# A depthwise convolution split by token parity: three half-length filters in place of 31 taps

## The chip, the cores and the metric

The kernel runs on one core of a Trainium2 chip. The metric is the device time of one launch in microseconds; the time given for a kernel is the median of its runs. The core's engines work side by side, each in the order of its own instruction stream: PE (TensorE, the matrix multiplier), DVE (VectorE), ACT (ScalarE), POOL (GpSimd) and SP (SyncE, which here only starts DMA transfers). They wait for each other through semaphores. SBUF is the core's working memory, PSUM the smaller memory into which PE writes its products.

## The reference

One layer of a decoder trunk over 1024 tokens with 1024 channels, in float32. Cut to what the change touches:

```python
h = rms_norm(x, attn_norm_w[l])
proj = h @ w_in[l]
q, k, v, u, g = jnp.split(proj, splits, axis=-1)
a = diff_attention(...)                       # 8 heads, q and k in two halves
y_a = rms_norm(a, ...) @ w_proj_attn[l]

u_a, u_b = jnp.split(u, 2, axis=-1)
c = causal_depthwise_conv(u_a * jax.nn.sigmoid(u_b), conv_w[l], conv_b[l])
c = jax.nn.silu(layer_norm(c, conv_ln_w[l], conv_ln_b[l]))
y_b = c @ w_proj_conv[l]

x = x + (g_a * y_a + g_b * y_b) @ w_out[l]
x = x + (silu(gate) * up) @ w_down[l]         # feed-forward, width 2816
```

The convolution works on each channel alone: token s of the output is the bias plus the sum over t = 0..30 of w[30-t] times token s-t of its input. The input is called u below, already gated (u_a times the sigmoid of u_b).

## The kernel before

**Layout and products.** Channels lie on the 128 partitions, tokens along the free axis, so that u and the convolution's output are eight tiles (c = 0..7) of 128 channels by 1024 tokens. A float32 matrix product is made of three matmuls on halves of the numbers: a high part (`whi`, a copy with rounding, ACT, line 120) and a low part (`wlo`, the difference, DVE line 125, or POOL line 131 while `low_by_pool` is set). Lines 168 to 170 are the three matmuls. Some products are formed as seven products of quarter blocks in place of eight (lines 981 and 489).

**The stages**, by the trace of the profiled execution: an opening up to 60 us; up to 270 us the first stage, in which u is projected and gated; up to 825 us attention, with the projections of q, k and the gates as filling; up to 1010 us the attention projection, the LayerNorm of the convolution and the convolution projection; up to 1100 us `w_out`; then the feed-forward part.

**How u is made.** `u_half` makes tile 0, `u_pair` (line 992) tiles 1 to 7. For each, PE writes seven products of 12 matmuls into three PSUM tiles a, b and c_, and between the products the results are drained: an ACT copy (lines 999 and following), DVE additions and multiplications (lines 1001, 1014, 1016, 1022), a multiplication on POOL (line 1018). The sums of weight blocks for the seven products are made by POOL (lines 962 to 965), which makes the low halves there too. The two halves of tile c (512 tokens each) go to a DRAM buffer `u_d[c]` by DMAs of SP (lines 1019, 1023).

**How the convolution is made.** `conv_load` (line 574) brings tile c back whole to SBUF (`us[c]`, two buffers). `conv_taps` returns 31 work items for a tile: `first_tap` on ACT (line 589: scale by the tap, add the bias, write `acc`), then 30 taps on DVE (line 595), each of which multiplies the first 1024-n tokens of u by a per-channel weight `cw` and adds them in place to the last 1024-n tokens of `acc`. For the first four tiles (`CONV_PSUM`) `acc` lies in PSUM, and after the last tap ACT copies it to an SBUF tile `done` (line 599); for the others it lies in SBUF. The finished tile goes to `c_d[c]` by a DMA of SP (line 601), tile 0 also to `cs_d` (line 603); the other tiles are added to `cs_d` in DRAM by an accumulating DMA of POOL (`add_tile`, line 579). In all DVE makes 8 x 30 = 240 taps.

**When.** The items wait in a list `bg`. In the first stage each step of the main loop puts 3.25 of them into the program (line 1242, `due += 3.25`), each behind DVE's last instruction so far; at the end of the stage `bg.until` (line 1078) puts in more until 127 remain, that is until tiles 0 to 3 are done and tile 4 is loaded. In attention the rest is spread over the steps (`share`, line 1443). The DMA that loads the next tile is placed in the list so that it comes just after the first tap of the tile before. A list scheduler of the language's framework then orders each engine's stream when the kernel is built.

**After attention** `ln_chunks` (line 1544) runs the LayerNorm for each half of the tokens: it loads `cs_d` and the eight `c_d` tiles (lines 1554 and 1556, nine DMAs a half), takes the mean by a matmul, subtracts (line 1570), squares, divides, gates, and writes the high and low halves into `cT_hi` and `cT_lo` (lines 1593, 1594), from which PE makes the convolution projection.

Of the kernel before, what the change touches and what calls it, by code (L numbers as in the profile page):

```python
# [10 lines left out]
F32 = mybir.dt.float32  # L11
# [20 lines left out]
NT = S // P  # L32
NKT = D // P
NSTD = 2
SUMS = ("T1", "T2", "T3", "T4")
SIDES = ("11", "12", "22", "S1", "S2", "S3", "S4")

# [20 lines left out]
def kernel(  # L58
# [157 lines left out]
    NROW = 64  # L216
    rows = ap.tile([NROW, P], F32, name="rows", bufs=1)
    col = {}
    at = [0]
# [26 lines left out]

    pvec = cst.tile([P, NROW], F32, name="pvec")
    cw = cst.tile([P, NKT, 32], F32, name="cw")
    neglam = cst.tile([P, 1], F32, name="neglam")
    lprod = ap.tile([P, 2, HD], F32, name="lprod", bufs=1)  # L250
    lsum = cst.tile([P, 2], F32, name="lsum")

    def pcol(key, k=0):
        c = col[key] + k
        return pvec[:, c : c + 1]

    def vectors():

        pt = pm()
        pe.transpose(pt[:, :NROW], rows[:], ident[:NROW, :NROW])  # L260
        dve.tensor_copy(pvec[:], pt[:, :NROW])
        dve.tensor_scalar(pcol("subln"), pcol("subln"), 1.0 - LAM_INIT, None, op0=ALU.mult)
        dve.tensor_scalar(pcol("kn"), pcol("kn"), -(HD ** -0.5), None, op0=ALU.mult)
        c_ = col["ln_w"]
        dve.tensor_scalar(pvec[:, c_ : c_ + 8], pvec[:, c_ : c_ + 8], -0.125, None, op0=ALU.mult)
        pt = pm()
        for k in range(NKT):
            pe.transpose(pt[:, k * 32 : k * 32 + CW], cwrow[:, k * P : (k + 1) * P], ident[:CW, :CW])
        dve.tensor_copy(
            cw[:, :, :CW], pt[:, : NKT * 32].rearrange("p (k t) -> p k t", t=32)[:, :, :CW]  # L270
        )
        for j in range(2):
            dve.tensor_tensor(lprod[:, j, :], lamt[:, 2 * j, :], lamt[:, 2 * j + 1, :], op=ALU.mult)
        dve.tensor_reduce(lsum[:], lprod[:], axis=AX.X, op=ALU.add)
# [296 lines left out]
    def conv_load(c):  # L571
        def go():
            us[c] = cv.tile([P, S], F32, tag="u", name=f"u{c}", bufs=2)
            nc.sync.dma_start(us[c][:], u_d[c][:])

        return go

    def add_tile(c):
        pool.dma_start(cs_d[:], c_d[c][:], accum_op=ALU.add, max_dma_last_dim=1024)

    def conv_taps(c):
        acc = []

        def first_tap():
            if c < CONV_PSUM:
                acc.append(pcv[0].tile([P, S], F32, tag="acc", name=f"acc{c}", bufs=1))
            else:
                acc.append(cv.tile([P, S], F32, tag="acc", name=f"acc{c}", bufs=1))
            act.activation(acc[0][:], us[c][:], AF.Identity, bias=pcol("conv_b", c), scale=cw[:, c, CW - 1 : CW])  # L589

        def tap(t):
            def go():
                n = CW - 1 - t
                a_ = acc[0][:, n:]
                dve.scalar_tensor_tensor(a_, us[c][:, : S - n], cw[:, c, t : t + 1], a_, op0=ALU.mult, op1=ALU.add)  # L595
                if t == 0:
                    if c < CONV_PSUM:
                        done = cv.tile([P, S], F32, tag="acc", name=f"done{c}", bufs=1)
                        act.copy(done[:], acc[0][:])
                        acc[0] = done  # L600
                    nc.sync.dma_start(c_d[c][:], acc[0][:])
                    if c == 0:
                        nc.sync.dma_start(cs_d[:], acc[0][:])
                if c > 1 and t == CW // 2:
# [5 lines left out]
        return [first_tap] + [tap(t) for t in range(CW - 2, -1, -1)]  # L610

    hT_hi = big.tile([P, NKT, S], F32R, tag="xhi", name="hT_hi")
    hT_lo = big.tile([P, NKT, S], F32R, tag="xlo", name="hT_lo")


    def u_half(c, w, sb, gemm=gemm_T):
        cs = slice(sb * 512, (sb + 1) * 512)
        ob = gemm_T(w[0], hT_hi, hT_lo, sb)
        sg = wp.tile([P, 512], F32, tag="sg", name=nm("sg"), bufs=2)
        act.activation(sg[:], ob[:], AF.Sigmoid)  # L620
        yield
        oa = gemm(w[1], hT_hi, hT_lo, sb)
        dve.tensor_tensor(sg[:], oa[:], sg[:], op=ALU.mult)
        nc.sync.dma_start(u_d[c][:, cs], sg[:])
# [368 lines left out]
    def u_pair(c, A, ahead):  # L993

        B = {(j, l): (hT_hi[:, KH[j], TOK[l]], hT_lo[:, KH[j], TOK[l]]) for j in range(2) for l in range(2)}
        a, b, c_ = acc(), acc(), acc()
        product(b, A["11"], B[0, 0], True)
        p1 = half("p1")
        act.copy(p1, b[:])
        product(a, A["12"], B[1, 0], True)  # L1000
        dve.tensor_tensor(p1, a[:], p1, op=ALU.add)
        act.activation(p1, p1, AF.Sigmoid)
        nxt = next(ahead, None)
        yield
        product(b, A["S2"], TS[2], False)
        u2 = half("u2")
        act.copy(u2, b[:])
        product(c_, A["S1"], TS[1], True)
        u3 = half("u3")
        act.copy(u3, c_[:])  # L1010
        next(ahead, None)
        yield
        product(b, A["S3"], TS[3], False)
        dve.tensor_tensor(u3, b[:], u3, op=ALU.add)
        product(c_, A["S4"], B[1, 1], False)
        dve.tensor_tensor(u2, c_[:], u2, op=ALU.add)
        act.activation(u2, u2, AF.Sigmoid)
        pool.tensor_tensor(u3, u3, u2, op=ALU.mult)
        nc.sync.dma_start(u_d[c][:, TOK[1]], u3)
        yield  # L1020
        product(b, A["22"], TS[4], False)
        dve.tensor_tensor(p1, b[:], p1, op=ALU.mult)
        nc.sync.dma_start(u_d[c][:, TOK[0]], p1)
        bg.todo.insert(max(0, len(bg.todo) - CW), conv_load(c))
        bg.add(conv_taps(c))
        next(ahead, None)
        yield
        return nxt

    def first_stage():  # L1030
# [203 lines left out]
    for _ in first_stage():  # L1234
# [309 lines left out]
    def ln_chunks(sb):  # L1544
# [6 lines left out]

        s1 = half("s")
        with after(last_at):
            nc.sync.dma_start(s1[:], cs_d[:, cs])
# [32 lines left out]
        for c in range(NKT):  # L1587
# [540 lines left out]
```

## Time and profile before

| what | value |
| --- | --- |
| runs (us) | 1737.25, 1738.83, 1738.94 (median 1738.83) |
| profiled execution: time, span of its profile | 1738.77 us, 1737.0 us |
| PE busy | 1717.4 us, 99% of the span |
| DVE busy | 1275.2 us, 73% |
| ACT busy | 863.3 us, 50% |
| POOL busy | 218.6 us, 13% (nearly all of it before 270 us) |
| share of the chain that ended last | PE 89%, DVE 4%, DMA 3%, ACT 2%, POOL 1%, issue 1% |
| the 240 convolution taps on DVE | 303.8 us, 1266 ns each |

The span is the profile's own stretch from the first to the last instruction; the profiled execution took 1.77 us more than that. Busy times of different engines overlap. The chain that ended last is followed back from the last instruction, at each step to what released it. "x -> y" times are of one execution; means of one instruction are in ns.

### The profile page before, as it was taken

How to read it: one execution, taken by the hardware profiler on the slowest of the kernel's cores; microseconds unless marked ns; L12 is line 12 of the kernel's file. 1: busy time of each engine (PE TensorE's matmuls, PEld its weight loads, DVE VectorE, ACT ScalarE, POOL GpSimd, SP SyncE). 2: the span in 40 equal slices, each digit the busy share in tenths (PEclk: the TensorE clock that was granted, in tenths of full speed). 3: DMA queues.
4: the chain of work that ended last, by engine and by line, in shares of the span. 5: the costliest groups of instructions: out<-in, count | busy, mean ns of one | idle time of the engine just before them, and what ended most of it. 6: DMA issues, size and time to landing. Idle time of an engine off the chain costs nothing.

```text
span 1737.0 us, 25860 instructions
## 1 busy us (share of the span) xinstructions
PE 1717.4 (99%) x9245; PEld 1478.8 (85%) x9245; DVE 1275.2 (73%) x2128; ACT 863.3 (50%) x1958; POOL 218.6 (13%) x207
## 2 busy tenths in 40 slices
PE   9999999999999999999999999999999999999999
PEld 7997879998998998988788877888888888888887
DVE  7575879898988888878687768966676666565554
ACT  6333335667777777765566325633333333333332
POOL 4997761000000000000000000000000000000000
PEclk9999999999999999999999999999999999999999
DMA  6343546435435344443963683235445444598663
GB/s 202 118 133 121 178 137 166 117 92 146 117 109 148 108 116 128 105 134 132 337 234 122 200 302 104 74 105 180 152 158 174 154 152 150 175 361 280 216 218 132
DMA packets 260453, 281.64 MB, mean 162 GB/s; under 512 B 16418, under 2 KB 181858, under 8 KB 260324
## 3 DMA queue, kind: packets, MB, share of 16 engines
q1 hardware_dynamic: 254352, 269.55, 48.1%
q0 software_dynamic: 5680, 9.39, 2.5%
q8 instruction: 73, 1.20, 0.3%
q10 hardware_dynamic: 292, 1.05, 0.2%
q14 instruction: 56, 0.46, 0.1%
HBM read 181.84 MB, written 85.50 MB: 154 GB/s over the span
## 4 chain that ended last, share of the span: by engine, by line
PE 89%; DVE 4%; DMA 3%; ACT 2%; POOL 1%; issue 1%; SPq 0%; POOLq 0%
PE acc L981 28%; PE acc L489 12%; PE pg L168 12%; PE pg L169 11%; PE pg L170 11%; PE wo L1843 2%; PE sc L1290 2%; PE sc L1289 2%; PE pT L1328 2%; DVE acc L595 1%; PE pW L168 1%; PE pW L169 1%; PE pW L170 1%; PE pg L1107 1%; DMA wraw<-in_w_in_dram 1%
## 5 line engine op out<-in xcount | busy, mean ns | idle before, releaser
L595 DVE SCALAR_TENSOR_TENSOR acc<-u,cw,acc 128x1023 f32<-128x1023 f32 (+14 forms) x240 | 303.8, 1266 | 14.6 <-ACT acc L589 12.1
L168 PE MATMUL pg<-whi,hT_hi 128*128 128x256 f32 x704 | 199.7, 285 | 0.6 <-DVE v L125 0.6
L170 PE MATMUL pg<-whi,hT_lo 128*128 128x256 f32 x704 | 200.0, 285 | 0.0
L169 PE MATMUL pg<-wlo,hT_hi 128*128 128x256 f32 x704 | 199.3, 284 | 0.0
L125 DVE TENSOR_TENSOR wlo<-draw,whi 128x1024 fp32r<-128x1024 f32 x75 | 91.8, 1224 | 86.0 <-ACT whi L120 84.3
L120 ACT CAST whi<-draw 128x1024 fp32r<-128x1024 f32 x75 | 79.1, 1055 | 129.5 <-PE acc L489 117.6
L168 PEld LDWEIGHTS pg<-whi,hT_hi 128*128 128x128 f32 x704 | 134.0, 191 | 2.4 <-DVE v L125 0.8
L169 PEld LDWEIGHTS pg<-wlo,hT_hi 128*128 128x128 f32 x704 | 134.2, 191 | 1.7
L170 PEld LDWEIGHTS pg<-whi,hT_lo 128*128 128x128 f32 x704 | 134.2, 191 | 1.8
L120 ACT CAST whi<-wraw 128x1024 fp32r<-128x1024 f32 x90 | 94.6, 1051 | 69.3 <-PE pg L169 29.3
L489 PE MATMUL acc<-wlo,whi 128*128 128x512 f32 x308 | 119.8, 389 | 0.0
L489 PE MATMUL acc<-whi,wlo 128*128 128x512 f32 x308 | 119.8, 389 | 0.0
L1296 ACT ACTIVATE E<-E,mn 128x640 f32<-128x640 f32 (+7 forms) x128 | 99.8, 780 | 31.1 <-DVE mn L1291 29.4
L168 PE MATMUL pg<-hT_hi,whi 128*128 128x512 f32 x288 | 114.4, 397 | 0.1
L169 PE MATMUL pg<-hT_lo,whi 128*128 128x512 f32 x288 | 113.7, 395 | 0.0
L170 PE MATMUL pg<-hT_hi,wlo 128*128 128x512 f32 x288 | 113.6, 395 | 0.0
L120 ACT CAST whi<-s 128x1024 fp32r<-128x1024 f32 x54 | 56.8, 1053 | 108.7 <-PE acc L981 104.9
L125 DVE TENSOR_TENSOR wlo<-wraw,whi 128x1024 fp32r<-128x1024 f32 x75 | 92.7, 1239 | 14.0 <-ACT whi L120 13.8
L1291 DVE CUSTOM_DVE_ANT_0 E<-sc,tb 128x512 f32<-128x512 f32 (+3 forms) x128 | 74.5, 587 | 32.4 <-PE pT L1328 15.9
L981 PE MATMUL acc<-h_hi,whi 128*128 128x512 f32 x240 | 93.4, 389 | 0.0
L981 PE MATMUL acc<-h_lo,whi 128*128 128x512 f32 x240 | 93.4, 389 | 0.0
L981 PE MATMUL acc<-h_hi,wlo 128*128 128x512 f32 x240 | 90.1, 389 | 0.0
(370 smaller groups left out, 4594.8 us busy)
## 6 DMA issues: line engine op xcount, KB each, us to landing
wraw<-in_w_gate_up_dram SPq DMA_DIRECT2D x44, 512.0 KB, 4.7
wraw<-in_w_in_dram SPq DMA_DIRECT2D x40, 512.0 KB, 4.4
qs<-qs SPq DMA_DIRECT2D x96, 128.0 KB, 2.4
wd<-in_w_down_dram SPq DMA_DIRECT2D x44, 256.0 KB, 3.1
tdT<-wd SPq DMA_DIRECT2D x88, 128.0 KB, 4.8
draw<-sdS SPq DMA_DIRECT2D x44, 256.0 KB, 4.0
draw<-tdT SPq DMA_DIRECT2D x44, 256.0 KB, 3.9
wraw<-in_w_in_dram SPq DMA_DIRECT2D x32, 256.0 KB, 3.3
```

The lines of the kernel that those rows point to most:

```text
L120: act.copy(dst, src)
L125: last_lo[0] = dve.tensor_tensor(dst, src, f32(hi), op=ALU.subtract).ins
L168: pe.matmul(o, lh, rh, start=start, stop=False)
L169: pe.matmul(o, lh, rl, start=False, stop=False)
L170: last_mm[0] = pe.matmul(o, ll, rh, start=False, stop=stop).ins
L489: m = pe.matmul(o[s_][i][:], l_[:, ts], r_[:, 512:], start=start and j + y_ == 0, stop=j == n - 1 and y_ == 2, skip_group_check=not start,)
L595: dve.scalar_tensor_tensor(a_, us[c][:, : S - n], cw[:, c, t : t + 1], a_, op0=ALU.mult, op1=ALU.add)
L981: last_mm[0] = pe.matmul(o[:], a_[x_][:, k, :], b_[y_][:, k, :], start=start and k + x_ + y_ == 0, stop=k == 3 and x_ == 1, skip_group_che ...
L1289: pe.matmul(o[:, :w], qh[:, qs], k, start=True, stop=False)
L1290: last_mm[0] = pe.matmul(o[:, :w], ql[:, qs], k, start=False, stop=True).ins
L1291: dve.tensor_tensor_reduce(e[:, ks], o[:, :w], tb[:, S - nk + c0 : S - nk + c0 + w], 1.0, mn[:, j : j + 1] if c0 else 3.0e38, ALU.add, ALU ...
L1296: act.activation(e[:, :nk], e[:, :nk], AF.Exp, bias=mn[:, j : j + 1], scale=-1.0, accum_out=l[:, j : j + 1])
```

## The change

The convolution is rewritten by token parity. Call x0 the even tokens of u and x1 the odd ones (512 each), h0 the 16 taps at even distance and h1 the 15 at odd distance, H a filter's result. Even output tokens need h0 on x0 plus h1 on the odd tokens one place earlier; odd output tokens need h1 on x0 plus h0 on x1. The latter is (h0+h1) on (x0+x1) minus h0 on x0 minus h1 on x1, so that three filters of 16, 15 and 16 taps on 512 tokens do the work of 31 taps on 1024.

For that, u is kept as two planes, even tokens first, then odd ones: the gating instructions read PSUM with a stride of two elements (`by_parity`) and write planes, the DMAs to `u_d` write 2 x 256 pieces, and `c_d` and `cs_d` are in planes too. `ln_chunks` loads planes, works on them, and writes `cT_hi` and `cT_lo` back in token order with a stride of two.

Per tile there are now 48 items in the place of 31: `start` (a DVE instruction `cws` that forms the negative sums of neighbouring taps, 128 x 16, and two ACT instructions on 512 tokens), 15 even taps, 14 odd taps, `mixed` (x0 += x1, DVE), `meet` (two DVE instructions; in the first four tiles also two ACT copies into the SBUF tile), 16 cross taps, the last followed by an ACT copy with scale -1 and the DMA to `c_d`. Each tap is a DVE instruction on at most 512 tokens. The first stage now puts in 4.9 items a step, and `bg.until` leaves 191. Once, a DVE memset and a DVE multiplication by 2 of the bias columns (128 x 8) come in.

```diff
-        def first_tap():
...
-            act.activation(acc[0][:], us[c][:], AF.Identity, bias=pcol("conv_b", c), scale=cw[:, c, CW - 1 : CW])
-
-        def tap(t):
+        def start():
+            pairs = cw[:, c, :].rearrange("p (i e) -> p i e", e=2)
+            dve.scalar_tensor_tensor(
+                cws[c % 2][:], pairs[:, :, 0], -1.0, pairs[:, :, 1], op0=ALU.mult, op1=ALU.subtract
+            )
...
+            act.activation(acc[0][:, :HS], x0(), AF.Identity, bias=pcol("conv_b", c), scale=h(0))
+            act.activation(acc[0][:, HS:], x1(), AF.Identity, scale=h(1))
+
+        def even(j):
             def go():
-                n = CW - 1 - t
-                a_ = acc[0][:, n:]
-                dve.scalar_tensor_tensor(a_, us[c][:, : S - n], cw[:, c, t : t + 1], a_, op0=ALU.mult, op1=ALU.add)
...
+                a_ = acc[0][:, j:HS]
+                dve.scalar_tensor_tensor(a_, x0(HS - j), h(2 * j), a_, op0=ALU.mult, op1=ALU.add)
...
+        def odd(j):
+            def go():
+                a_ = acc[0][:, HS + j :]
+                dve.scalar_tensor_tensor(a_, x1(HS - j), h(2 * j + 1), a_, op0=ALU.mult, op1=ALU.add)
+                if c > 1 and j == 8:
                     with after(last_of(mybir.EngineType.DVE)):
                         add_tile(c - 1)
...
+        def mixed():
+            dve.tensor_tensor(x0(), x0(), x1(), op=ALU.add)
+
+        def meet():
...
+            if inside:
+                y = cv.tile([P, S], F32, tag="acc", name=f"done{c}", bufs=1)
+                act.copy(y[:, HS:], b_)
...
+                act.copy(y[:, 0:1], a_[:, 0:1])
+                dve.tensor_tensor(y[:, 1:HS], a_[:, 1:], b_[:, : HS - 1], op=ALU.add)
+                dve.scalar_tensor_tensor(a_, a_, twice, b_, op0=ALU.subtract, op1=ALU.add)
+                d.extend((a_, y))
+            else:
+                dve.scalar_tensor_tensor(x1(), a_, twice, b_, op0=ALU.subtract, op1=ALU.add)
+                dve.tensor_tensor(a_[:, 1:], a_[:, 1:], b_[:, : HS - 1], op=ALU.add)
+                d.extend((x1(), acc[0]))
+
+        def cross(j):
+            def go():
...
+                dve.scalar_tensor_tensor(a_, x0(HS - j), cws[c % 2][:, 15 - j : 16 - j], a_, op0=ALU.mult, op1=ALU.add)
+                if j == 15:
+                    act.activation(y[:, HS:], d_, AF.Identity, scale=-1.0)
+                    nc.sync.dma_start(c_d[c][:], y[:])
...
     def u_pair(c, A, ahead):
...
-        act.copy(p1, b[:])
+        act.copy(planes(p1), by_parity(b))
         product(a, A["12"], B[1, 0], True)
-        dve.tensor_tensor(p1, a[:], p1, op=ALU.add)
+        dve.tensor_tensor(planes(p1), by_parity(a), planes(p1), op=ALU.add)
...
-        nc.sync.dma_start(u_d[c][:, TOK[0]], p1)
-        bg.todo.insert(max(0, len(bg.todo) - CW), conv_load(c))
+        nc.sync.dma_start(plane_rows(u_d[c], 0), planes(p1))
+        bg.todo.insert(max(0, len(bg.todo) - NTAP + 1), conv_load(c))
...
-        bg.until((NKT - CONV_PSUM) * (CW + 1) - 1)
+        bg.until((NKT - CONV_PSUM) * NTAP - 1)
...
-        due += 3.25
+        due += 4.9
...
     def ln_chunks(sb):
...
-                nc.sync.dma_start(cc[c], c_d[c][:, cs])
+                nc.sync.dma_start(planes(cc[c]), plane_rows(c_d[c], sb))
...
-            split_hi(cT_hi[:, c, cs], z[:])
-            split_lo(cT_lo[:, c, cs], z[:], cT_hi[:, c, cs])
+            hi, lo = [by_parity(t_[:, c, cs]) for t_ in (cT_hi, cT_lo)]
+            split_hi(hi, planes(z))
+            split_lo(lo, planes(z), hi)
```

What the change moves shows in the streams of DVE and SP. First DVE in the first stage, the second half of tile 0; `u_…` made from `pg_…` at L125 and `p_…`, `u_…` made from `acc_…` at L1001 and L1014 are drains of PE's results, `acc_989` is the convolution's accumulator. Before:

```order
L125 TENSOR_TENSOR u_117_1374<-pg_1324,p_116_1373 128x512
L595 SCALAR_TENSOR_TENSOR acc_989<-u_987,cw,acc_989 128x1006
L595 SCALAR_TENSOR_TENSOR acc_989<-u_987,cw,acc_989 128x1005
L125 TENSOR_TENSOR u_122_1448<-pg_1398,p_121_1447 128x512
L595 SCALAR_TENSOR_TENSOR acc_989<-u_987,cw,acc_989 128x1004
L595 SCALAR_TENSOR_TENSOR acc_989<-u_987,cw,acc_989 128x1003
L595 SCALAR_TENSOR_TENSOR acc_989<-u_987,cw,acc_989 128x1002
L125 TENSOR_TENSOR u_127_1514<-pg_1464,p_126_1513 128x512
```

The same stretch now, with `mixed` (L637) and `meet` (L647, L648) between the drains (L127, the old L125), and the cross taps at L659:

```order
L127 TENSOR_TENSOR u_117_1389<-pg_1339,p_116_1388 128x512
L637 TENSOR_TENSOR u_991<-u_991 128x512
L629 SCALAR_TENSOR_TENSOR acc_994<-u_991,cw,acc_994 128x500
L629 SCALAR_TENSOR_TENSOR acc_994<-u_991,cw,acc_994 128x499
L629 SCALAR_TENSOR_TENSOR acc_994<-u_991,cw,acc_994 128x498
L127 TENSOR_TENSOR u_122_1469<-pg_1419,p_121_1468 128x512
L647 TENSOR_TENSOR done_1413<-acc_994,done_1413 128x511
L648 SCALAR_TENSOR_TENSOR acc_994<-acc_994,pvec,done_1413 128x512
L659 SCALAR_TENSOR_TENSOR acc_994<-u_991,cws_113,acc_994 128x512
L659 SCALAR_TENSOR_TENSOR acc_994<-u_991,cws_113,acc_994 128x511
L659 SCALAR_TENSOR_TENSOR acc_994<-u_991,cws_113,acc_994 128x510
L127 TENSOR_TENSOR u_127_1537<-pg_1487,p_126_1536 128x512
```

The scheduler has put `mixed` three rows ahead of the last odd taps; between two drains stand four to six half taps or combining steps where two or three whole taps stood.

Second, SP's queue late in the first stage, where it loads weights (`wraw`), stores u, and stores a convolution tile (`c_d`). Before:

```order
L601 DMA c_d_141<-done_2028 128x1024
L945 DMA wraw_2270<-in_w_in_dram 128x8x128
L1023 DMA u_d_136<-p_200_1998 128x512
L945 DMA wraw_2272<-in_w_in_dram 128x8x128
L1023 DMA u_d_137<-p_218_2145 128x512
```

Now:

```order
L662 DMA c_d_143<-done_1959 128x1024
L1083 DMA u_d_138<-p_200_2045 256x1x256
L1005 DMA wraw_2335<-in_w_in_dram 128x8x128
L1005 DMA wraw_2337<-in_w_in_dram 128x8x128
L1083 DMA u_d_139<-p_218_2199 256x1x256
```

The store of u that stood between the two weight loads now stands ahead of both, and is cut into 256 pieces.

Third, DVE at the end of attention, where tile 6 ends and tile 7 starts. `E`, `mn` and `rl` belong to the softmax, `pl` and `wlo` are low halves. Before, tile 7's first taps stand in one group:

```order
L1303 RECIPROCAL rl_5_7385<-l_8186 128x2
L1304 SCALAR_TENSOR_TENSOR rl_8199<-rl_5_7385,neglam,l_8186 128x1
L1306 SCALAR_TENSOR_TENSOR E_8187<-E_8193,rl_8199,E_8187 128x512
L125 TENSOR_TENSOR pl_8098<-pT_8101,ph_8097 128x128
L595 SCALAR_TENSOR_TENSOR acc_8105<-u_6215,cw,acc_8105 128x1023
L595 SCALAR_TENSOR_TENSOR acc_8105<-u_6215,cw,acc_8105 128x1022
L595 SCALAR_TENSOR_TENSOR acc_8105<-u_6215,cw,acc_8105 128x1021
L125 TENSOR_TENSOR pl_8232<-pT_8235,ph_8231 128x3x128
```

Now tile 6's last cross tap and tile 7's `cws` and first taps stand singly among them:

```order
L612 SCALAR_TENSOR_TENSOR cws_114<-cw 128x16
L1351 ISA E_8353,mn_8345<-sc_8354,tb_7511 128x512
L1351 ISA mn_8345 128x1
L659 SCALAR_TENSOR_TENSOR u_4349<-u_4349,cws_113 128x497
L127 TENSOR_TENSOR pl_8257<-pT_8260,ph_8256 128x128
L1363 RECIPROCAL rl_5_7535<-l_8346 128x2
L1364 SCALAR_TENSOR_TENSOR rl_8359<-rl_5_7535,neglam,l_8346 128x1
L1366 SCALAR_TENSOR_TENSOR E_8347<-E_8353,rl_8359,E_8347 128x512
L127 TENSOR_TENSOR pl_8257<-pT_8321,ph_8256 128x2x128
L1351 ISA E_8409,mn_8407<-sc_8410,tb_8405 128x512
L1351 ISA mn_8407 128x1
L622 SCALAR_TENSOR_TENSOR acc_8207<-u_6353,cw,acc_8207 128x511
```

Between the last tap of tile 6 and the first of tile 7 there are seven other rows.

More of the change, by code (lines that the diff above doesn't have):

```diff
@@ L34 @@
 NSTD = 2
+HS = S // 2
+NTAP = 48
 SUMS = ("T1", "T2", "T3", "T4")
@@ L248 @@
     cw = cst.tile([P, NKT, 32], F32, name="cw")
+    cws = [cst.tile([P, 16], F32, name=f"cws{e}") for e in range(2)]
     neglam = cst.tile([P, 1], F32, name="neglam")
@@ L579, in add_tile, with by_parity @@
         pool.dma_start(cs_d[:], c_d[c][:], accum_op=ALU.add, max_dma_last_dim=1024)
-    def conv_taps(c):
-        acc = []
-        def first_tap():
[L585 to L589, printed above, removed]
-        def tap(t):
-            def go():
-                n = CW - 1 - t
-                a_ = acc[0][:, n:]
[L595 to L604, printed above, removed]
+    def by_parity(t_):
+        return t_[:].rearrange("p (m e) -> p e m", e=2)
@@ L608, in tap @@
             return go
-        return [first_tap] + [tap(t) for t in range(CW - 2, -1, -1)]
+        def mixed():
+            dve.tensor_tensor(x0(), x0(), x1(), op=ALU.add)
+        def meet():
+            a_, b_ = acc[0][:, :HS], acc[0][:, HS:]
+            twice = pvec[:, B2 + c : B2 + c + 1]
+            if inside:
+                y = cv.tile([P, S], F32, tag="acc", name=f"done{c}", bufs=1)
+                act.copy(y[:, HS:], b_)
+                b_ = y[:, HS:]
+                act.copy(y[:, 0:1], a_[:, 0:1])
[8 more added lines that the diff above has]
+            def go():
+                d_, y = d
+                a_ = d_[:, j:]
+                dve.scalar_tensor_tensor(a_, x0(HS - j), cws[c % 2][:, 15 - j : 16 - j], a_, op0=ALU.mult, op1=ALU.add)
+                if j == 15:
+                    act.activation(y[:, HS:], d_, AF.Identity, scale=-1.0)
+                    nc.sync.dma_start(c_d[c][:], y[:])
+                    if c == 0:
+                        nc.sync.dma_start(cs_d[:], y[:])
+            return go
+        return (
+            [start] + [even(j) for j in range(1, 16)] + [odd(j) for j in range(1, 15)]
+            + [mixed, meet] + [cross(j) for j in range(16)]
+        )
     hT_hi = big.tile([P, NKT, S], F32R, tag="xhi", name="hT_hi")
```

42 lines of the change are left out of this document (28 added, 14 removed).

## The prediction

> **What bounds the kernel now.** I read the page's busy times and chain first, then the busy times by stage, then what PE waits for.
>
> ```profile
> span 1737.0 us, 25860 instructions
> PE 1717.4 (99%) x9245; PEld 1478.8 (85%) x9245; DVE 1275.2 (73%) x2128; ACT 863.3 (50%) x1958; POOL 218.6 (13%) x207
> PE 89%; DVE 4%; DMA 3%; ACT 2%; POOL 1%; issue 1%; SPq 0%; POOLq 0%
> ```
>
> PE is busy for all but 19.6 us. The stages that the change touches (us, then busy time and instruction count of PE, PEld, DVE, ACT, POOL, granted clock, DMA share, GB/s):
>
> ```profile
> 60.00:270.00 210.00, 206.00 (x1134) 177.81 (x1133) 148.95 (x138) 77.08 (x120) 160.44 (x100) 0.99 0.48 147
> 270.00:825.00 555.00, 553.28 (x3758) 508.84 (x3757) 478.53 (x1023) 387.06 (x1274) 24.21 (x72) 1.00 0.43 122
> 825.00:1010.00 185.00, 184.15 (x826) 151.73 (x825) 131.52 (x219) 93.54 (x148) 0.60 (x1) 1.00 0.64 214
> ```
>
> PE idles 4.0 us in the first stage, 1.7 in attention, 0.85 up to the end of the convolution projection: 6.6 us in all. That is the most that work taken from DVE can return, apart from what hides inside a busy PE. PE's waits in these stages, as total, times, longest:
>
> ```profile
> PE acc L981 <- POOL wlo L131: 4.0, 1, 4.0
> PE pg L168 <- DVE v L125: 0.6, 1, 0.6
> PE pg L168 <- DVE gt L1637: 0.5, 1, 0.5
> PE sc L1289 <- DVE mn L1291: 0.2, 1, 0.2
> ```
>
> None of them names a tap. The 4.0 us are the first stage's whole idle time, and POOL owes them to a weight load:
>
> ```profile
> 205.24 12.16 DMA wraw<-in_w_in_dram
> 217.53 1.29 POOL L962 TENSOR_TENSOR s<-wraw 128x512 f32<-128x512 f32 x1 [8.33 <-DMA wraw<-in_w_in_dram]
> 227.50 2.35 POOL L131 TENSOR_TENSOR wlo<-wraw,whi 128x1024 fp32r<-128x1024 f32 x1
> ```
>
> POOL stood for 8.33 us until a transfer of 12.16 us landed, and PE goes on after POOL's low half at 229.85. No engine was short of time there, so the convolution's length is not what holds PE.
>
> **The taps.** What they cost, and the two rows that give the price of a half (start, time, engine, operation):
>
> ```profile
> L595 DVE SCALAR_TENSOR_TENSOR acc<-u,cw,acc 128x1023 f32<-128x1023 f32 (+14 forms) x240 | 303.8, 1266 | 14.6 <-ACT acc L589 12.1
> 295.19 1.22 DVE L808 TENSOR_TENSOR qkraw<-qkraw,r 128x1024 f32<-128x1024 f32 x1
> L1014 DVE TENSOR_TENSOR u<-acc,u 128x512 f32<-128x512 f32 x7 | 4.8, 688 | 6.9 <-PE acc L981 6.9
> 34.25 2.74 DVE L715 SCALAR_TENSOR_TENSOR xt<-xt,r,anw_b 128x512 f32<-128x512 f32 x4
> ```
>
> 512 tokens less shorten an addition by 1.22 - 0.69 = 0.53 us, so a half tap takes at most 1.266 - 0.53 = 0.74 us; four instructions of the same operation on 512 elements took 2.74, 0.685 each. I take 0.72, nearer to the tap's own row. Per tile 30 x 1.266 = 38.0 us go. In their place come 15 + 14 + 16 = 45 half taps and one instruction of `meet` of that kind, 46 x 0.72 = 33.1 us, two additions (`mixed`, the other half of `meet`) of 0.69, and `cws` on 128 x 16 at 0.17 (row below): 34.7 us. DVE saves 3.3 us a tile (2.4 with 0.74, 4.9 with 0.685), 26 us in eight tiles (19 to 39): 2% of its busy time, where halving the arithmetic might suggest much more, because each instruction has a fixed part of about 0.16 us (2 x 0.69 - 1.22), paid 19 more times a tile. About 13 us of it lie in the first stage, where DVE has 61 us idle anyway, and 13 in attention, where PE's waits on DVE that a freer DVE could shorten are 0.6 and 0.2. I count -0.8 us there, bounds -1.7 and 0.
>
> **ACT.** The rows, and one of 512 tokens:
>
> ```profile
> L589 ACT ACTIVATE acc<-u,pvec,cw x8: 1201/1223/1243, 73.1 to 691.0; 128x1024 f32<-128x1024 f32 x8
> L599 ACT COPY done<-acc x4: 1002/1014/1021, 126.2 to 310.3; 128x1024 f32<-128x1024 f32 x4
> 677.83 0.69 ACT L640 ACTIVATE sgg<-pg,pvec 128x512 f32<-128x512 f32 x1 [3.31 <-PE pg L170]
> 289.73 0.59 ACT L120 CAST v<-pg 128x512 fp32r<-128x512 f32 x1
> ```
>
> The first four tiles had 1.22 + 1.01; they now have two starts of 0.69, a copy of 0.59, one of a single column (at most 0.2) and the negation of 0.69: 2.86, +0.6. The others go from 1.22 to 3 x 0.69 = 2.07, +0.85. Together +6 us on an engine that idles half the time. It stands on a path only where one tile follows another on the single `acc` buffer:
>
> ```profile
> 684.52 1.25 DVE L595 SCALAR_TENSOR_TENSOR acc<-u,cw,acc 128x994 f32<-128x994 f32 x1
> 691.00 1.23 ACT L589 ACTIVATE acc<-u,pvec,cw 128x1024 f32<-128x1024 f32 x1
> 692.62 3.91 DVE L595 SCALAR_TENSOR_TENSOR acc<-u,cw,acc 128x1023 f32<-128x1023 f32 x3
> ```
>
> From the last tap's end (685.77) the store and the next start take 5.2 us; the negation puts 0.7 before the store. With seven rows between the two tiles on DVE there is other work for that time, and DVE's next taps are waited for by no one; ACT, standing for the buffer, holds the exponentials behind it by up to 0.7 us in each of three crossings. PE has shown no wait for that, so 0 here, bound +2.
>
> **DVE against POOL in the first stage.** `cws` and `mixed` read two SBUF operands. Before, the taps of these tiles read one, since `acc` lies in PSUM. What happens to such an instruction while POOL works:
>
> ```profile
> 278.03 2.41 POOL L131 TENSOR_TENSOR wlo<-wraw,whi 128x1024 fp32r<-128x1024 f32 x1 [15.50 <-ACT whi L120]
> 278.51 1.97 DVE L658 TENSOR_TENSOR r<-r,t 128x16 f32<-128x16 f32 x1
> 280.94 2.42 POOL L131 TENSOR_TENSOR wlo<-wraw,whi 128x1024 fp32r<-128x1024 f32 x1
> 281.57 2.88 DVE L808 TENSOR_TENSOR qkraw<-qkraw,r 128x1024 f32<-128x1024 f32 x1
> L656 DVE SCALAR_TENSOR_TENSOR t<-v,t 128x16 f32<-128x16 f32 (+1 forms) x23 | 3.8, 167 | 0.1
> L595 DVE SCALAR_TENSOR_TENSOR acc<-u,cw,acc 128x1023 f32<-128x1023 f32 (+14 forms) x99 | 125.9, 1271 | 11.8 <-ACT acc L589 9.4
> ```
>
> A 128 x 16 instruction took 1.97 us where its neighbour line 656 takes 0.17, and it ended when POOL's did (280.4); the addition at 281.57 took 2.88 in place of 1.22 and ended one addition after POOL's end at 283.36. The 99 taps beside a POOL that is busy 160 of 210 us took 1271 ns, as everywhere. So each of the eight new instructions may stand for up to 2.4 us, on average half of that by three quarters, 0.9: 7 us of DVE, which eats half of the stage's saving. [...]
>
> What of it reaches PE? Drains have a window:
>
> ```profile
> 221.65 0.39 PE L981 MATMUL acc<-T2l,whi 128*128 128x512 f32 x1
> 225.05 0.39 PE L981 MATMUL acc<-hT_hi,whi 128*128 128x512 f32 x1
> ```
>
> 15 matmuls start in 3.40 us, 0.227 each, so that a product of 12 lasts 2.7 us, and a result is to be read in that time before its PSUM tile is written again. A drain of 0.69 behind one half tap in progress leaves 1.3 us; a `mixed` that stands for more than that just ahead of a drain delays PE by the rest, at most 1.1. In the first place that the streams show, three half taps stand between `mixed` and the next drain, which are delayed with it. I count +1.0 us over the stage: one bad meeting out of eight. Bounds 0 and +6.
>
> **Strided PSUM reads, planes and DMAs.** 30 DVE drains (four in each of seven pairs, two for tile 0) and 23 on ACT now read every second element. No row of before has such a read. If the stride is free they cost nothing; if each takes as long as 1024 elements, DVE pays 30 x 0.53 = 16 us and ACT 23 x 0.46 = 11. I take 0, nearest to the drains' own row of 688 ns, since the count of elements is the same. The stores of u and the LayerNorm's loads are cut into pieces of 1 KB:
>
> ```profile
> q1 hardware_dynamic: 254352, 269.55, 48.1%
> L168 PE MATMUL pg<-cT_hi,whi x128: 389/389/395, 921.9 to 1008.3; 128*128 128x512 f32 x128
> 920.64 0.69 DVE L125 TENSOR_TENSOR cT_lo<-lnz,cT_hi 128x512 fp32r<-128x512 f32 x1 [1.67 <-ACT cT_hi L120]
> 944.78 1.46 DVE L125 TENSOR_TENSOR cT_lo<-lnz,cT_hi 128x512 fp32r<-128x512 f32 x2
> ```
>
> Packets (count, MB, share of 16 engines' span) cost 0.481 x 1737 x 16 / 254352 = 53 ns at a mean of 1060 bytes. Nine loads of a half give 9 x 128 = 1152 packets more, between 0 (the bytes are the same) and 1152 x 53 / 16 = 3.8 us. I take 0.5, as the bytes are the same. PE first reads `cT` at 921.9, three matmuls per channel tile, and so the eighth tile at 921.9 + 7 x 3 x 0.227 = 926.7, while it was ready at 921.33: 5.4 us to spare in the first half. In the second half PE is only just behind (the last low half at 946.2). The strided writes cost nothing if free, or 0.53 us each. I count +0.3 on PE, bounds 0 and +5.
>
> **The sum.** First stage +1.0, attention -0.8, LayerNorm +0.3: +0.5 on the profiled execution's 1738.77 (span 1737.0 and 1.77 around it; the median of the runs is 1738.83). Forecast: 1739 us, no change. I call a change within 0.2% (3.5 us) none, about what a measurement of this kernel can tell.
>
> **The rivals.**
>
> D, faster. The two weight loads at 203 to 217 us collide less: the store of u no longer stands between them, and DVE and ACT release the buffers at other times. If POOL's wait of 8.33 us shrinks by half, PE's 4.0 go, and with attention's 0.8 the time is 1734. For it: those 4.0 us hang on one slow transfer. Against: the loads still come behind two stores, and nothing makes them start earlier.
>
> B, slower. The eight instructions with two SBUF operands meet POOL where PE is close: POOL is busy three quarters of the stage, and the end of its chain at 225 us is PE's one wait. [...]
>
> C, slower. The strided reads take double time. An ACT copy of 1.05 in place of 0.59, an addition of 1.22 in place of 0.69 and a half tap in progress make 1.94 of the 2.7 us of a window; one pair in which ACT or DVE is late by more loses about 0.7 us, seven pairs 5: 1744. [...]
>
> E, slower. The LayerNorm comes late in its second half: 3.8 us of packets, or strided writes at double time; PE waits +4 to +5 near 946: 1743.
>
> F, slower. At the crossings of tiles in attention ACT stands behind the later store and exponentials come late: three times 0.7 to 2 us, up to +5, 1744.
>
> **How the numbers follow.** No change 0.36, since idle PE time leaves at most 6.6 us to win and the cover is large. D 0.28. B 0.14, C 0.09, E 0.08, F 0.05. So faster 0.28, same 0.36, slower 0.36. The range reaches from D with a little more (1733) to a sum of two of the slower cases (1748).
>
> **What would show it.** In the profile after: half taps of 0.69 to 0.74 us and DVE busy some 15 to 35 us less; the drains at lines 1061 to 1082 at 0.69 (C wrong) or over 1 us (C right); `cws` at lines of 0.17 or near 2 us, and `mixed` above 0.69 (B); PE's wait for POOL's low half near 225 us, still 4 us or gone (D); PE's first matmuls on `cT` without waits (E wrong). The prediction is wrong if PE's busy time itself changes, as by a new order of its stream, or if PE's waits in the first stage grow beyond 10 us.

## The result, and the profile after

The changed kernel takes 1747.64 us (median of 4 runs, 1747.03 to 1749.08) against 1738.11 us before: a ratio of 1.0052, with a 95% interval of 1.004 to 1.0065. It is slower by 0.5%, 9.5 us, and that is clear of the 0.2% within which the prediction would have called it no change.

The page after, with the same three lines as before:

```profile
span 1747.3 us, 26028 instructions
PE 1728.1 (99%) x9245; PEld 1480.0 (85%) x9245; DVE 1262.4 (72%) x2282; ACT 867.3 (50%) x1978; POOL 219.6 (13%) x207
PE 92%; DVE 2%; DMA 2%; ACT 2%; POOL 1%; issue 1%; SPq 0%; ACTq 0%; POOLq 0%; DVEq 0%
```

The span is 10.3 us longer, and PE is *busy* for 10.7 us longer, with the same 9245 instructions. PE does not wait more: its idle time is 19.2 us, before 19.6. By stages:

```profile
60.00:270.00 210.00, 205.11 (x1105) 175.08 (x1104) 151.61 (x201) 76.67 (x119) 161.79 (x100) 0.98 0.48 145
270.00:825.00 555.00, 554.30 (x3783) 511.72 (x3782) 462.20 (x1112) 390.69 (x1292) 23.39 (x71) 1.00 0.45 124
825.00:1010.00 185.00, 184.43 (x821) 150.80 (x820) 131.51 (x217) 95.23 (x152) 1.45 (x3) 1.00 0.65 213
```

And PE's longest waits in them:

```profile
PE acc L1041 <- POOL wlo L133: 3.8, 1, 3.8
PE pg L170 <- ACT jk L861: 0.6, 2, 0.4
PE pg L170 <- DVE gt L1698: 0.4, 1, 0.4
```

So matmuls themselves are slower, and most of all where nothing was changed: in the feed-forward part. Both kernels keep PE wholly busy there from 1150 to 1500 us. Before, PE runs 1546 matmuls in that stretch (one that crosses a border counts); behind it the rows of the matmuls that read the tile `T1h` there and, earlier, attention's result `aTh`:

```profile
1150.00:1500.00 350.00, 350.00 (x1546) 289.89 (x1545) 230.75 (x344) 120.34 (x166) 0.00 (x0) 1.00 0.50 159
```

```profile
L981 PE MATMUL acc<-T1h,whi x80: 389/389/389, 1148.2 to 1514.7; 128*128 128x512 f32 x80
L168 PE MATMUL pg<-aTh,whi x128: 388/389/501, 828.4 to 921.2; 128*128 128x512 f32 x128
```

After, it runs 1519, at the same granted clock of 1.00; behind it the rows by tile:

```profile
1150.00:1500.00 350.00, 350.00 (x1519) 284.89 (x1518) 229.69 (x344) 118.60 (x164) 0.00 (x0) 1.00 0.49 154
```

```profile
L1041 PE MATMUL acc<-T1h,whi x80: 392/394/398, 1151.7 to 1524.8; 128*128 128x512 f32 x80
L170 PE MATMUL pg<-aTh,whi x128: 387/393/498, 829.5 to 923.8; 128*128 128x512 f32 x128
L170 PE MATMUL pg<-cT_hi,whi x128: 387/389/399, 924.5 to 1010.9; 128*128 128x512 f32 x128
```

27 matmuls fewer at 0.226 us are 6.1 us in this stretch alone. The tile rows (minimum, median, maximum in ns) say which matmuls: the median of those that read `T1h` went from 389 to 394, of those that read `aTh` from 389 to 393, and those that read `cT_hi` took 389 as before. DVE, ACT and DMA are as busy beside them as before (230 us, 119 and a share of 0.49).

What changed for these tiles is their place. Among the addresses of the built program, every tile allocated from the left end of SBUF (weights `whi` and `wlo`, `hT`, `cT`) lies 128 bytes further on than before: the two new tiles `cws0` and `cws1`, 64 bytes a partition each, stand ahead of them in the pool `cst`. The tiles allocated from the right end (`T1` to `T4` of the feed-forward part, `aTh`, `aTl`, `mTh`) did not move. I sorted all matmuls of 512 columns by the address of the moving operand less that of the weights, modulo 256, and took the mean time from one matmul's start to the next of the same size from the trace:

| kernel | difference 0 | difference 128 |
| --- | --- | --- |
| before | 5556 in the program; 227.5 ns | none |
| after | 3936; 228.0 ns | 1620; 232.7 ns |

1620 x (232.7 - 227.5) = 8.4 us, and 3936 x 0.5 = 2.0 us for the others, most of it in the feed-forward part, where they alternate with the slow ones: 10.4 us, the whole difference of the spans.

### The profile page after: what moved, and what is told of

Read it like the earlier page. It is cut to its first block, busy times and chain, and to the rows that moved or that the text cites. A ratio compares the mean times of both kernels' runs of the same rounds, so it can differ in the third digit from the quotient of the medians.

```text
span 1747.3 us, 26028 instructions
## 1 busy us (share of the span) xinstructions
PE 1728.1 (99%) x9245; PEld 1480.0 (85%) x9245; DVE 1262.4 (72%) x2282; ACT 867.3 (50%) x1978; POOL 219.6 (13%) x207
## 4 chain that ended last, share of the span: by engine, by line
PE 92%; DVE 2%; DMA 2%; ACT 2%; POOL 1%; issue 1%; SPq 0%; ACTq 0%; POOLq 0%; DVEq 0%
PE acc L1041 28%; PE pg L170 12%; PE pg L172 12%; PE pg L171 12%; PE acc L495 12%; PE wo L1904 3%; PE sc L1350 2%; PE sc L1349 2%; PE pT L1388 2%; PE pW L172 1%; PE pW L171 1%; PE pW L170 1%; PE pg L1167 1%; PE pQ L876 1%; DMA wraw<-in_w_in_dram 1%
## 5 line engine op out<-in xcount | busy, mean ns | idle before, releaser
L127 DVE TENSOR_TENSOR wlo<-draw,whi 128x1024 fp32r<-128x1024 f32 x75 | 91.8, 1224 | 86.4 <-ACT whi L122 80.4
L127 DVE TENSOR_TENSOR wlo<-wraw,whi 128x1024 fp32r<-128x1024 f32 x75 | 95.0, 1271 | 13.2 <-ACT whi L122 12.9
L622 DVE SCALAR_TENSOR_TENSOR acc<-u,cw,acc 128x511 f32<-128x511 f32 (+14 forms) x120 | 89.1, 742 | 15.6 <-ACT acc L617 8.1
```

Source lines behind the costliest of these rows:

```text
L127: last_lo[0] = dve.tensor_tensor(dst, src, f32(hi), op=ALU.subtract).ins
L622: dve.scalar_tensor_tensor(a_, x0(HS - j), h(2 * j), a_, op0=ALU.mult, op1=ALU.add)
```

## The experiments

Theory P (places): the 9.5 us come from the 128 bytes by which the left tiles moved, and the convolution has no part in them. Theory C: they come from the new convolution, its strided reads, waits and order; then experiment 1 stays at 1747.6 us. The first four kernels tell these apart.

**1. The changed kernel in the old places.** The sums are kept in the spare tile `pad_sm`, which the kernel has and nobody uses:

```diff
-    sm.tile([P, 32], F32, name="pad_sm", bufs=1)
+    pad_sm = sm.tile([P, 32], F32, name="pad_sm", bufs=1)
...
-    cws = [cst.tile([P, 16], F32, name=f"cws{e}") for e in range(2)]
+    cws = [pad_sm[:, 16 * e : 16 * e + 16] for e in range(2)]
```

> The changed kernel with its two weight-sum tiles (2 x 64 bytes a partition) cut out of the spare tile pad_sm, which is there already, so that every other SBUF tile lies at the address it has in the kernel before. Nothing that is computed changes. Theory P (places): of the 5556 matmuls of 512 columns, 1620 read a moving operand and weights whose addresses differ by 128 modulo 256 in the changed kernel, none in the kernel before, and each of these starts 5.8 ns later (232.6 in place of 226.8); 1620 x 5.8 = 9.4 us is the whole loss, so 1738.2 us here, within 1737 and 1740, and the matmuls of the feed-forward part back at 226.7 ns. [...]

Measured: 1737.93 us, ratio to before 0.9988 (0.9978 to 0.9998). In its profile the matmuls are back; the page's busy times, the stretch of the feed-forward part and the tile:

```profile
PE 1716.1 (99%) x9245; PEld 1479.0 (85%) x9245; DVE 1261.5 (73%) x2282; ACT 868.7 (50%) x1978; POOL 219.5 (13%) x207
```

```profile
1150.00:1500.00 350.00, 350.00 (x1546) 289.91 (x1545) 232.57 (x348) 120.32 (x166) 0.00 (x0) 1.00 0.50 160
```

```profile
L1041 PE MATMUL acc<-T1h,whi x80: 389/389/389, 1147.7 to 1514.2; 128*128 128x512 f32 x80
```

With the same convolution, and the same number of instructions on each engine, the loss is gone. Theory C falls.

**2. The kernel before, moved.** One unused tile ahead of `neglam`, and nothing else:

```diff
+    pad = cst.tile([P, 32], F32, name="pad")
     neglam = cst.tile([P, 1], F32, name="neglam")
```

> The kernel before with nothing but an unused tile of 128 bytes a partition ahead of neglam, where the changed kernel has its weight sums. Theory P: the same 1620 matmuls are misplaced, 1738.1 + 9.4 = 1747.5 us. Theory C: 1738.1 us, no change.

Measured: 1747.83 us, ratio 1.0046 (1.0034 to 1.0058). A tile that no instruction touches costs as much as the whole change did. In the stretch from 1150 to 1500 us its PE runs 1518 matmuls:

```profile
1150.00:1500.00 350.00, 350.00 (x1518) 284.82 (x1517) 227.85 (x340) 118.84 (x163) 0.00 (x0) 1.00 0.48 152
```

```profile
L982 PE MATMUL acc<-T1h,whi x80: 392/394/398, 1150.5 to 1523.6; 128*128 128x512 f32 x80
```

**3. The changed kernel with the right end moved as well.**

```diff
-    edge.tile([P, 56], F32, name="pad_right")
+    edge.tile([P, 24], F32, name="pad_right")
```

> The changed kernel with the spare tile at the right end of SBUF (pad_right) made 128 bytes smaller, so that the tiles allocated from the right move by 128 bytes too and again agree with those from the left modulo 256, at other addresses than before. Theory P, if the difference between the two operands counts: 1738.2 us. If the absolute address modulo 512 counts instead: 1747.6 us or more. Theory C: 1747.6 us.

Measured: 1738.59 us, ratio 0.9998 (0.999 to 1.0007), and matmuls of 227.5 ns. Two shifts of 128 bytes cancel: what counts here is not the address of a tile, but the difference between a matmul's two operands. One question stays open: nearly all of the 1620 stand next to others with the same difference, so whether a matmul's own weights count or those of the next one, loaded in the meantime, can't be told from these runs.

**4. Other distances.** The unused tile of the second kernel with 64, 32, 192 and 256 bytes.

> The kernel before with an unused tile of 64 bytes in the same place, so that the same 1620 matmuls have operands that differ by 64 or 192 modulo 256. Theory P with any difference costing the same: 1747.5 us. With a cost in proportion to the difference: about 1742.8 us. If only multiples of 128 count: 1738.1 us. Theory C: 1738.1 us.

> The kernel before with an unused tile of 32 bytes: 1344 matmuls whose moving operand lies 224 modulo 256 past their weights, 276 with 32. If any difference costs some 6 ns a matmul: 1620 x 6 = 9.7 us, 1748 us. If the cost grows with the distance: 1741 us or less.

> The kernel before with an unused tile of 192 bytes: now 1344 matmuls have a difference of 64 and 276 one of 192, the other way round than with 64 bytes. There 64 cost 2.2 ns and 192 6.3 ns a matmul. If the cost depends on moving minus weights in this way: 1344 x 2.2 + 276 x 6.3 = 4.7 us, 1743 us. If it depends on the tiles and not on the difference: 1748 to 1750 us as with 64 bytes.

> The kernel before with an unused tile of 256 bytes in the place of the 128: the left and the right tiles again differ by a multiple of 256. If the rule is modulo 256: no change, 1738.5 us within 2. If what costs is any tile in that place, or a shift of the left tiles as such: 1747 to 1750 us.

Measured. 1344 of the matmuls read the moving operand from the right end and the weights from the left, 276 the other way round, so each tile gives two differences:

| unused tile | time, us | ratio to before (95%) | difference: ns from start to start | matmuls, 1150 to 1500 us |
| --- | --- | --- | --- | --- |
| 32 bytes | 1750.53 | 1.0066 (1.005 to 1.0081) | 224: 233.2; 32: 233.0 | 1516 |
| 64 | 1750.71 | 1.006 (1.0049 to 1.0072) | 192: 233.3; 64: 229.2 | 1517 |
| 128 | 1747.83 | 1.0046 (1.0034 to 1.0058) | 128: 232.7 | 1518 |
| 192 | 1746.84 | 1.0047 (1.0033 to 1.0061) | 64: 230.3; 192: 233.3 | 1523 |
| 256 | 1739.42 | 1.0002 (0.9991 to 1.0012) | 0: 227.5 | 1546 |

A shift of 256 bytes changes nothing, and of the differences tried below that each costs 5 to 6 ns a matmul, save 64, which costs 1.7 and 2.8 (229.2 and 230.3 for 227.5). The rows are of different sessions: the kernel before took 1738.85 us beside 64 and 128 bytes, 1739.78 beside 32 and 192, and 1739.44 beside 256. With 192 bytes I had expected 4.7 us more than before by a rule on the difference alone, which is 1744.5 us on that session's kernel before; the 1746.84 is above it, in part because the 1344 matmuls took 230.3 and not 229.2. The difference is most of the cause and not all of it.

**5. Sums made early.** With the places settled, what is left of the convolution's own effect? The first experiment's profile has a `cws` of 4.14 us beside POOL, and PE idle for 6.7 us in the first stage in place of 4.0. Here the sums of tiles 0 to 4 are made once, by an instruction with one operand in PSUM, in a tile that moves the left side by 256 bytes:

```diff
-    cst.tile([P, 16], F32, name="pad_left")
+    cws5 = cst.tile([P, 5, 16], F32, name="cws5")
...
+        dve.scalar_tensor_tensor(
+            cws5[:],
+            cw[:].rearrange("p k (i e) -> p k i e", e=2)[:, :5, :, 0],
+            -1.0,
+            pt[:, : NKT * 32].rearrange("p (k i e) -> p k i e", i=16, e=2)[:, :5, :, 0],
...
-            dve.scalar_tensor_tensor(
+            if c > 4:
+              dve.scalar_tensor_tensor(
                 cws[c % 2][:], pairs[:, :, 0], -1.0, pairs[:, :, 1], op0=ALU.mult, op1=ALU.subtract
```

> The changed kernel in places that agree modulo 256 (all left tiles 256 bytes further than before), with the weight sums of tiles 0 to 4 made once at the start by one DVE instruction that reads one operand from PSUM, so that the cws instructions of the first stage, of which one stood 4.14 us beside POOL in the changed kernel with the old places, are gone. If those waits cost PE what the first stage lost there (idle 6.7 us in place of 4.0): 1738 - 2.7 = about 1735.5 us, at least below 1737. If the loss of the first stage has another cause: 1738 us.

Measured: 1741.6 us, ratio 1.0017 (1.0008 to 1.0025). Neither expectation came: the first stage idles less, though not by the mechanism expected, and something behind it lost more. First the kernel of experiment 1, the first stage and three stretches at the start of attention:

```profile
60.00:270.00 210.00, 203.32 (x1104) 173.93 (x1103) 150.79 (x200) 76.42 (x119) 161.32 (x100) 0.99 0.47 145
...
318.00:322.00 4.00, 4.00 (x32) 3.78 (x31) 1.51 (x4) 2.36 (x5) 1.03 (x1) 1.00 0.15 47
322.00:326.00 4.00, 4.00 (x33) 3.92 (x32) 4.00 (x12) 3.78 (x20) 0.00 (x0) 1.00 0.89 129
326.00:330.00 4.00, 4.00 (x35) 3.95 (x34) 4.00 (x12) 2.58 (x8) 0.00 (x0) 1.00 0.01 2
```

Then the kernel with the sums made early, and behind it its new wait:

```profile
60.00:270.00 210.00, 205.12 (x1118) 175.92 (x1117) 147.28 (x200) 77.66 (x124) 161.67 (x100) 0.99 0.49 147
...
318.00:322.00 4.00, 2.04 (x11) 1.19 (x9) 4.00 (x9) 3.87 (x20) 0.00 (x0) 0.97 0.89 129
322.00:326.00 4.00, 3.48 (x17) 3.42 (x17) 4.00 (x13) 3.78 (x22) 0.00 (x0) 0.50 0.03 6
326.00:330.00 4.00, 4.00 (x23) 3.92 (x23) 3.14 (x7) 1.42 (x5) 0.00 (x0) 0.67 0.01 2
```

```profile
PE sc L1359 <- DVE mn L1361: 2.0, 2, 1.2
```

PE idles 4.9 us in the first stage, 1.8 less than in experiment 1. That isn't shown to come from `cws`: the changed kernel and the kernels of experiments 3 and 7 have every `cws` and the same order of PE's stream as experiment 1, and idle 4.9, 5.9 and 5.8 us there. And the longest `cws` delayed nobody. Behind it DVE stood for ACT in any case, in experiment 1 (first two rows) for 4.77 us, and here, without it, for 9.06 (last row):

```profile
137.37 4.14 DVE L612 SCALAR_TENSOR_TENSOR pad_sm<-cw 128x16 f32<-128x16 f32 x1
146.28 0.76 DVE L622 SCALAR_TENSOR_TENSOR acc<-u,cw,acc 128x511 f32<-128x511 f32 x1 [4.77 <-ACT acc L617]
146.88 0.76 DVE L631 SCALAR_TENSOR_TENSOR acc<-u,cw,acc 128x511 f32<-128x511 f32 x1 [9.06 <-ACT acc L626]
```

What was lost behind it is clearer. The list scheduler, given other instructions, wrote another order: the first score product stands nine rows earlier in PE's stream. PE then waits for DVE's and ACT's part of the softmax, idles 2.0 us of the 4 from 318 to 322, and from there its granted clock is 0.50 until about 328.6. The three rows count 51 matmuls where experiment 1 has 100. Summed over the trace, the matmuls between 300 and 350 us start some 6 us later than their usual distances, in experiment 1 less than 1: two microseconds of waiting cost about six. The expectation failed in its mechanism, since `cws` was not what held PE, and it had no term for a new order.

**6. Less DVE work.** All but one of the cross taps of each tile are left out of the kernel of experiment 1:

```diff
+                if j == 15:
                     dve.scalar_tensor_tensor(a_, x0(HS - j), cws[c % 2][:, 15 - j : 16 - j], a_, op0=ALU.mult, op1=ALU.add)
```

> The changed kernel with the old places and 15 of the 16 cross taps of each tile left out (the convolution's odd tokens are then incomplete): 120 half taps, 89 us of DVE, less. If DVE's work is covered by PE, as forecast: 0 to 2 us faster, 1736 to 1738 us. If a shorter convolution is worth something that its 154 more instructions hid: 1733 us or less.

Measured: 1743.16 us, ratio 1.0023 (1.0014 to 1.0031): neither expectation. The page's busy times and PE's waits:

```profile
PE 1717.7 (99%) x9245; PEld 1480.4 (85%) x9245; DVE 1190.6 (68%) x2162; ACT 867.0 (50%) x1978; POOL 219.5 (13%) x207
```

```profile
PE acc L1042 <- POOL wlo L133: 3.8, 1, 3.8
PE sc L1350 <- DVE mn L1352: 1.8, 1, 1.8
PE acc L1042 <- ACT u L1068: 1.6, 1, 1.6
```

DVE is busy 71 us less than in experiment 1 and nothing gets faster; a wait of 3.8 us behind POOL stays (3.8 in the changed kernel, 4.6 in experiment 1). The order of PE's stream changed too, so the whole times don't isolate DVE's work. A stretch without new waits comes closer: from 330 to 825 us, with the kernels lined up by the work that PE has done (as described in the next section), this one gains 2.7 us on the kernel before, and the four with all taps (experiments 1, 3, 5 and the next) gain 1.7 to 3.1. There the taps left out buy nothing. The loss lies again in a new order, with waits at the first scores (the first score product comes 6.9 us earlier than in experiment 1) and in the first stage. 1.2 us of it lie before 55 us, ahead of the first tap, and those I cannot explain.

**7. The identity matrix.** The operands of the 680 transposes of 128 columns differ by 192 modulo 256 in the kernel before and in experiment 1. (Not in every kernel so far, as the expectation has it: 552 of them lie at 64 in the changed kernel and in experiment 2, and at 128, 160 and 0 in those of experiment 4 with 64, 32 and 192 bytes.) Spare tiles put their matrix in agreement, in the kernel of experiment 1 and in the kernel before:

```diff
-    cst.tile([P, 16], F32, name="pad_left")
+    cst.tile([P, 32], F32, name="pad_left")
...
+    cst.tile([P, 48], F32, name="pad_more")
     neglam = cst.tile([P, 1], F32, name="neglam")
```

> The changed kernel in the old places modulo 256, with the identity matrix of the transposes moved too (spare tiles of 64 more bytes ahead of it and 192 behind), so that the 680 transposes of 128 columns, which so far differ by 192 modulo 256 in every kernel, also agree. If the rule of the 512-column matmuls holds for them at some 3 to 6 ns each: 2 to 4 us faster than the same kernel without it, 1734 to 1736 us. If a matmul of 128 columns has time to spare for it, as those of 256 columns have (118 to 119 ns with and without a difference): 1738 us.

> The kernel before with the identity matrix placed in the same way, nothing else changed. With the rule holding for the transposes: 1734.5 to 1736.5 us; without: 1738.5 us.

Measured: 1738.35 us, ratio 0.9998 (0.9989 to 1.0007), and 1739.04 us, ratio 0.9997 (0.9988 to 1.0005). The transposes take 109 ns from start to start with and without, and at each of the other differences just named. The difference costs nothing at 128 columns, nor at 256 (118.8 ns with a difference of 128, 119.5 without).

No kernel beats the kernel before by more than the 0.2% that the prediction calls no change. The best is experiment 1, about 10 us below the changed kernel and at 0.9988 of the kernel before.

## Where the prediction was wrong, and where right, point by point

It forecast 1739 us and no change, with 0.36 for slower. The kernel became 0.5% slower. The time lies just inside the range (1733 to 1748), and that is luck: the upper end stands for two of the slower rivals at once, none of them came at its price, and no rival describes what happened.

**The step that failed** is the sum: "First stage +1.0, attention -0.8, LayerNorm +0.3: +0.5". It has no term for the rate of PE itself. `cws` was costed as a DVE instruction (0.17 us, and more beside POOL), and the line of the diff that allocates it was costed at nothing, although all tiles behind it at the left end of SBUF move by its size. The missing term measured +8 to +10 us (experiments 1 and 2), more than all others together. The kernel showed where to look: `pad_left`, `pad_right` and `pad_sm` are tiles that no instruction uses, and with them all 5556 matmuls of 512 columns agreed; in the program built without the three, 1872 of them differ. The prediction did name a change of PE's busy time as what would make it wrong, but looked for it in the order of PE's stream.

The other terms can be read from experiment 1, where the places are as before. Idle times of fixed windows mislead a little, since the same window doesn't hold the same work. So I also lined the kernels up by PE's work: each matmul counts the usual distance of its size (227.3 ns at 512 columns, 120 at 256, 109 for a transpose), and compared are the times at which the same amount is done. Each figure is of one profiled execution.

- *Taps.* Taken at 0.72 us. Rows of the changed kernel's first stage, and behind them the ACT copy of before (line 999):

```profile
L622 DVE SCALAR_TENSOR_TENSOR acc<-u,cw,acc 128x511 f32<-128x511 f32 (+14 forms) x57 | 42.5, 746 | 9.7 <-ACT acc L617 8.1
L612 DVE SCALAR_TENSOR_TENSOR cws<-cw 128x16 f32<-128x16 f32 x5 | 6.4, 1283 | 0.0
L637 DVE TENSOR_TENSOR u<-u 128x512 f32<-128x512 f32 x3 | 3.8, 1264 | 0.0
L1061 DVE TENSOR_TENSOR p<-acc,p 128x512 f32<-128x512 f32 x7 | 4.8, 687 | 2.0 <-ACT p L1059 1.5 <-PE acc L1041 0.4
L1059 ACT COPY p<-acc 128x512 f32<-128x512 f32 x7 | 4.1, 582 | 8.3 <-PE acc L1041 8.3
L999 ACT COPY p<-acc x7: 577/582/589, 116.8 to 233.9; 128x512 f32<-128x512 f32 x7
```

  0.746 here, just above the bound of 0.74, and DVE is busy 12.8 us less in all, where the forecast had 26 less 7.
- *First stage, DVE against POOL* (rival B). The waiting on DVE was sized well: five `cws` and three `mixed` took 6.4 + 3.8 = 10.2 us where 5 x 0.17 + 3 x 0.69 = 2.9 would do, 7.3 us more, forecast 7. That a `mixed` also holds POOL for its own 0.69 us, which the slower cases at the upper end of the range count in, no run shows: beside two of the stage's three in the changed kernel POOL's instructions took 1.77 us for a median of 1.30 and 2.85 for 2.41 (so did another of that kind with no `mixed` beside it), and beside the third POOL stood for `wraw`. What either does to PE is not shown. The stage costs more than the forecast +1.0 (bounds 0 and +6): PE idles 6.7 us in experiment 1 for 4.0 before, and lined up it falls 3.7 us behind. But PE's waits there name POOL's low half (4.6 us for 4.0) and two ACT copies (1.6), none of them DVE, and experiment 5 shows the longest `cws` without effect. Which of the new waits come from the new order and which from meetings of DVE and POOL stays open.
- *Attention.* Forecast -0.8 (bounds -1.7 and 0). PE is busy 554.73 of 555 us in experiment 1, before 553.28: -1.45. Lined up, it catches up 3.3 us between 270 and 825 us (2.9 and 4.1 in experiments 3 and 7): mis-sized, beyond the bound.
- *Strided PSUM reads* (rival C) cost nothing that shows. The drains that read every second element take 687 ns on DVE and 582 on ACT; the drain on DVE quoted of before took 688, and the same ACT copy before 582. That holds for these reads by DVE and ACT at a stride of two; no other stride was tried.
- *LayerNorm* (rival E) was in time: PE is busy 184.54 us in experiment 1 for 184.15, and lined up it wins 0.9 us there, forecast +0.3. The strided writes cost DVE nothing (688 ns for 687) and ACT a little (658 for 616), which held no one.
- *The weight load* (rival D) came later and not earlier. The second of the two started at 205.24 us before, at 207.68 in the changed kernel and at 208.80 in experiment 1, and took about 12.2 us each time; PE's wait behind POOL was 4.0, 3.8 and 4.6 us.
- *Crossings of tiles* (rival F) did not hold PE: its waits from 270 to 1010 us are 0.8 us in experiment 1, before 1.9.

Lined up, the stages of experiment 1 make +3.7 - 3.3 - 0.9 = -0.5 us, as the spans do (1736.5 and 1737.0); by its runs it is 0.3 to 3.8 us below the kernel before (0.9978 to 0.9998). For the rewritten convolution by itself "no change" was right, but by a loss and a gain that are each some four times as large as forecast and cancel. That, too, is partly luck.

## What to carry to other kernels

A new tile is part of a change's cost even if it holds 128 bytes a partition: here it moved every tile behind it at the left end of SBUF, and that cost 8 to 10 us (experiments 1 and 2). Where PE is the bound, list the addresses of the built program and compare, for each large group of matmuls, the moving operand and the weights; a spare tile that looks like nothing may be there to keep them in step. When a stage that a change doesn't touch gets slower at the same instruction count and clock, look at where its data lies before looking at who waits for whom.

## What the runs showed of the hardware

- In these kernels a float32r matmul of 512 columns started its successor after 227.5 ns where its two operands agreed modulo 256 bytes in SBUF (228.0 in the changed kernel), and after 232.7 to 233.3 where they differed by 32, 128, 192 or 224; at 64 it took 229.2 and 230.3. Float32r matmuls of 256 columns took 118.8 ns with a difference of 128 and 119.5 without, and the transposes of 128 columns (float32) 109 ns at every difference that occurred. What in the memory does this was not tried.
- In some places a stop of PE of a few microseconds was followed by a lower granted clock and so paid for again. Before, after the wait near 226 us:

```profile
226.00:230.00 4.00, 0.10 (x1) 0.11 (x1) 3.96 (x4) 0.63 (x1) 4.00 (x4) 0.94 0.46 131
230.00:234.00 4.00, 4.00 (x12) 3.19 (x13) 2.66 (x3) 0.10 (x1) 2.18 (x1) 0.63 0.45 131
```

  The second row has 12 matmuls where 4 us hold some 17.6: the wait of 4.0 us cost more than 5. The granted clock was 0.50 from 230.0 to 232.9 us and 1.00 from 234 on. In experiment 5 a wait of 2.0 us, in two pieces, was followed by 0.50 for almost 7 us, and PE was busy for 2.04 of the 4 us before it, while a wait of 1.2 us at 221 us in experiment 1 left the clock at 1.00. What sets the clock back, and for how long, was not tried further. The prediction priced PE's waits without this.
